# Seven products of 2x2 blocks in place of eight in half of the FFN's up projection

## The chip, the cores and the metric

The kernel runs on one core of a Trainium2 chip. The metric is device time in microseconds: from the first to the last instruction of the program on that core, lower is better. TensorE does the matrix products, VectorE and ScalarE work on elements and read the products out of PSUM, GpSimd does small moves, and SyncE (SP) issues most of the DMAs.

## What is computed

One layer of a hybrid causal decoder on 512 prompt tokens and 8 x 4 sample tokens, 544 in all, in fp32. The part that matters here is the last third of it, the ConvFFN:

```python
x = x + g1 * (jnp.concatenate([a_out, o], axis=-1) @ p['w_out'])
h2 = rms_norm(x, p['norm_ffn_g']) * (1 + sc2) + sh2
u, f_tail = causal_dwconv(f_prev, h2 @ p['w_up'], p['ffn_conv_w'], p['ffn_conv_b'])
gate, val = jnp.split(u, 2, axis=-1)
x = x + g2 * ((jax.nn.silu(gate) * val) @ p['w_down'])
```

`w_up` is 2048 x 11264, `w_down` 5632 x 2048, and the convolution has three taps along time.

## The kernel before

Channels lie on partitions, tokens on the free axis in two halves of 272 columns (256 of the prompt, 16 of the samples). A K tile is 128 input channels; the model width has 16. Every fp32 product is made of three fp32r products: `split` (L340) writes the rounded operand with ScalarE (hi) and the remainder with VectorE (lo), and `mm3` (L201) adds hi x hi, hi x lo and lo x hi in PSUM for both token halves, six matmuls of 128x128 weights and 272 columns. So a K tile of one output tile costs six matmuls.

Weights come through SP's queue in units of 512 KB: `load_w` (L190) fills one of three `raw_w` buffers with eight K tiles of an output tile, `split_w` (L195) splits four of them at once into `whi` and `wlo`, which have three buffers each. `mm_unit` (L208) is one load, two splits and 48 matmuls; `mm_pair_unit` (L219) does the same for four K tiles of two output tiles.

The FFN (from L840) has 44 pairs of tiles, gate tile f and value tile 44 + f. For each tile `up_conv` (L863) runs two units over the 16 K tiles into one accumulator of two banks, copies it to `us` with ScalarE (L874, L875), lets GpSimd copy the last columns to `tails`, and convolves: ScalarE makes `ca` (L879), VectorE adds two taps (L881). `up_pair` (L886) then applies SiLU to the gate tile, multiplies (L896, L902) and splits the result into `ahi` and `alo`, which the down projection reads. The first pair goes through `mm_pair_unit` over four units of a reordered copy `w_up0`, so that it uses each K tile of h2 as soon as it is there. The loop (L925 to L934) takes four pairs as a chunk. `down` (L908) for the chunk before stands behind the second pair of the next: eight loads, 16 output tiles of 24 matmuls, each added to x by `gated_add` (L332). The FFN's accumulators alternate between two pools, `ps_main` and `psf`, four buffers of two banks in all. `shift_cache` (L854) issues 128 copies of the attention cache from HBM to HBM on SP's queue, one behind every second load.

Between the output projection and the FFN (L827 to L837), the sum of squares becomes `rstd2`, each of the 16 K tiles goes through `modulated` (L324: a product on VectorE, scale and shift on ScalarE, two small steps on VectorE, hi on ScalarE, lo on VectorE), and the last `ada_stage` (L257) makes the gate of the FFN from 16 loads in `RAW_G` buffers.

The order in each engine's queue is not written out by hand: the framework lays the program out ahead of time with a model of the engines, and takes what comes first in the program where several instructions are ready. Queues run in that order on the chip.

Of the kernel before, what the change touches and what calls it, by code (L numbers as in the profile page):

```python
# [14 lines left out]
ALU = mybir.AluOpType  # L15
# [43 lines left out]
RAW_G = 7  # L59
# [59 lines left out]
def build(ctx, tc, A):  # L119
# [12 lines left out]
    hlp = pool("hlp")  # L132
    halfp = pool("halfp", bufs=2)
    ps_main = pool("ps_main", bufs=2, space=PSUM)
# [25 lines left out]
    # ------------------------------------------------------------ constants  # L160
# [25 lines left out]
    # ------------------------------------------------------------ weights  # L186
    def raw_tile():
        return wp.tile([P, 1024], F32, name="raw_s", bufs=RAW_S)
# [67 lines left out]
    # ------------------------------------------------------------ adaLN  # L256
# [39 lines left out]
    # ------------------------------------------------------------ norms  # L296
# [27 lines left out]
    def modulated(xk, rstd, sc, sh, hi, lo, xn):  # L324
        nc.vector.tensor_tensor(xn, xk, rstd, op=ALU.mult)  # L325
        nc.scalar.activation(pv(xn), pv(xn), AF.Identity, bias=modT[:, sh, 0:1], scale=modT[:, sc, 0:1])
        nc.vector.tensor_tensor(sv4(xn), sv4(xn), per_batch(modT[:, sc, 1:9]), op=ALU.mult)
        nc.vector.tensor_tensor(sv4(xn), sv4(xn), per_batch(modT[:, sh, 1:9]), op=ALU.add)
        nc.scalar.copy(hi, xn)
        nc.vector.tensor_tensor(lo, xn, hi.bitcast(F32), op=ALU.subtract)  # L330
# [19 lines left out]
    # ------------------------------------------------------------ norm and first projections  # L350
# [5 lines left out]
    b1 = mid.enter_context(ExitStack())  # L356
    wk = pool("wk", bufs=4, to=b1)
# [70 lines left out]
    # ------------------------------------------------------------ q, k, v and prompt attention  # L428
# [140 lines left out]
    # ------------------------------------------------------------ conv group  # L569
# [54 lines left out]
    # ------------------------------------------------------------ sample attention  # L624
# [147 lines left out]
    # ------------------------------------------------------------ output projection  # L772
# [34 lines left out]
    op = pool("op", bufs=4, to=o1)  # L807
    x2.append(half_tile())
    nc.scalar.dma_start(x2[1], A["xT"][:, 8:16])
    ssum2 = op.tile([P, 2, HALF], F32, name="ssum", bufs=1)  # L810

# [20 lines left out]
    h2hi, h2lo = hl_tiles()  # L832
    for k in range(KT):
        xn = op.tile([P, 2, HALF], F32, name="xn", bufs=XN)
        modulated(x2[k // 8][:, k % 8], rstd2, SC2 + k, SH2 + k, h2hi[:, k], h2lo[:, k], xn)
# [4 lines left out]
    fs = ctx.enter_context(ExitStack())  # L840
    psf = pool("psf", bufs=2, space=PSUM, to=fs)
# [4 lines left out]
    turn = [0]  # L846

    def ffn_ps():
        turn[0] += 1
        if turn[0] % 2:  # L850
            return main_ps()
        return psf.tile([P, 2, 512], F32, name="acc2")
# [10 lines left out]
    def up_conv(m, st_in, tails, slot, ps=None):  # L863
        if ps is None:
            ps = ffn_ps()
            for h in range(2):
                ins = mm_unit(ps, A["w_up"][m, h], h2hi, h2lo, 8 * h, h == 0, h == 1)
                if h:
                    shift_cache(ins)
# [4 lines left out]
        nc.scalar.copy(us[:, 2:USEG].rearrange("p (c n) -> p c n", c=2), pv(ps))  # L874
        nc.scalar.copy(us[:, USEG:].rearrange("p (c b w) -> p c b w", c=2, w=2 + DT)[:, :, :, 2:], sv4(ps))  # L875
# [10 lines left out]
    def up_pair(f, st_in, tails, j):  # L886
        pss = (None, None)
        if f == 0:
            pss = (ffn_ps(), ffn_ps())
            for q in range(4):  # L890
                mm_pair_unit(pss, A["w_up0"][q], h2hi, h2lo, 4 * q, q == 0, q == 3)
        gt = up_conv(f, st_in, tails, 2 * j, pss[0])
        vl = up_conv(FT + f, st_in, tails, 2 * j + 1, pss[1])
# [9 lines left out]
        hi = fp.tile([P, 2, HALF], F32R, name="ahi", bufs=6)  # L903
        lo = fp.tile([P, 2, HALF], F32R, name="alo", bufs=6)
# [3 lines left out]
    def down(c, last):  # L908
        for mp in range(8):
# [3 lines left out]
            for j in range(2):  # L913
                m = 2 * mp + j
                hi, lo = split_w(raw[:, j])
                ps = ffn_ps()
# [8 lines left out]
    for c in range(NCHUNK):  # L925
# [133 lines left out]
```

## Time and profile before

| | |
|---|---|
| median of 3 runs | 2702.55 us (2698.33 to 2708.47) |
| span of the profiled execution | 2703.5 us |
| TensorE busy | 2658.7 us (98%) |
| VectorE busy | 1353.2 us (50%) |
| ScalarE busy | 1026.9 us (38%) |
| GpSimd busy | 114.2 us (4%) |
| mean granted TensorE clock | 0.991 |

The page of the profile gives busy time of each engine and, in 40 slices of the span, its busy share. The chain of waits follows the work that ended last back through what released it. The views by line and shape give the mean duration of an instruction and the idle time of its engine before it; the timeline gives instructions in order of time, and the windows sum the engines' busy time in a stretch and show the granted clock there (1.00 is 2.4 GHz, 0.50 is 1.2 GHz).

### The profile page before, as it was taken

The page shows a single profiled execution, that of the slowest core. Times are in us where ns is not written, and L with a number is a line of the kernel's source. Part 1 is how long each engine was busy: PE and PEld are TensorE (multiplying, and loading weights), DVE is VectorE, ACT ScalarE, POOL GpSimd, SP SyncE. Part 2 cuts the span into 40 slices and gives each one's busy share as a digit, 9 for nine tenths or more (in the row PEclk, how much of TensorE's full clock was granted, in tenths as well). Part 3 has the DMA queues.
Part 4 walks back from the last instruction along what each step waited for, and adds up shares of the span by engine and source line. Part 5 has one row for each costly group of instructions (what it writes and reads, how often), then busy time and mean ns, then how long its engine had stood idle before and what let it go on. Part 6 is the DMA issues. An engine that isn't in the chain of part 4 may idle for free.

```text
span 2703.5 us, 51563 instructions
## 1 busy us (share of the span) xinstructions
PE 2658.7 (98%) x21601; PEld 2437.8 (90%) x21601; DVE 1353.2 (50%) x2584; ACT 1026.9 (38%) x1977; POOL 114.2 (4%) x448
## 2 busy tenths in 40 slices
PE   7999999999999999999999999999999999999999
PEld 5878677768777799799999999999999999999999
DVE  5678654744674243644444443444443534444444
ACT  4355454445446432533332323232323233332322
POOL 0000000000000000000000000000000000000000
PEclk8999999999999999999999999999999999999999
DMA  9874557676655442455555455454554555545544
GB/s 350 280 274 156 190 196 262 224 260 221 237 204 192 146 182 87 157 186 180 171 182 180 165 182 186 165 182 165 187 176 170 180 172 181 181 165 182 178 172 153
DMA packets 119129, 517.49 MB, mean 191 GB/s; under 512 B 15728, under 2 KB 25584, under 8 KB 116080
## 3 DMA queue, kind: packets, MB, share of 16 engines
q1 hardware_dynamic: 103744, 494.98, 52.6%
q10 hardware_dynamic: 15152, 19.22, 2.0%
q8 instruction: 169, 2.77, 0.4%
q14 instruction: 64, 0.52, 0.1%
HBM read 503.18 MB, written 144.92 MB: 240 GB/s over the span
## 4 chain that ended last, share of the span: by engine, by line
PE 96%; DMA 2%; DVE 1%; ACT 0%; issue 0%; ACTq 0%; DVEq 0%; SPq 0%
PE acc L205 85%; PE x L270 4%; PE x L701 2%; PE x L652 2%; DMA raw_s<-w_ada 1%; PE m L510 1%; PE m L440 1%; PE m L475 1%; PE m L472 1%; PE m L493 0%; PE acc L322 0%; DMA half<-xT 0%; DVE xn L325 0%; DMA raw_s<-kT_c 0%; PE m L502 0%; DMA small<-c_small 0%
## 5 line engine op out<-in xcount | busy, mean ns | idle before, releaser
L205 PE MATMUL acc<-hhi,whi 128*128 128x272 f32 x4608 | 975.0, 292 | 4.5 <-ACT hhi L341 2.3
L205 PE MATMUL acc<-hhi,wlo 128*128 128x272 f32 x4608 | 964.8, 290 | 0.0
L205 PE MATMUL acc<-hlo,whi 128*128 128x272 f32 x4608 | 961.5, 290 | 0.4 <-DVE hlo L330 0.2
L341 ACT CAST whi<-raw_w 128x512 fp32r<-128x512 f32 x752 | 466.2, 621 | 1304.1 <-PE acc L205 1256.5
L342 DVE TENSOR_TENSOR wlo<-raw_w,whi 128x512 fp32r<-128x512 f32 x752 | 517.6, 689 | 749.7 <-ACT whi L341 738.9
L205 PEld LDWEIGHTS acc<-hhi,whi 128*128 128x128 f32 x4608 | 724.9, 189 | 56.6 <-issue 40.0
L205 PEld LDWEIGHTS acc<-hlo,whi 128*128 128x128 f32 x4608 | 725.8, 189 | 22.9 <-issue 18.5
L205 PEld LDWEIGHTS acc<-hhi,wlo 128*128 128x128 f32 x4608 | 723.0, 189 | 22.6 <-issue 20.9
L205 PE MATMUL acc<-alo,whi 128*128 128x272 f32 x1408 | 292.0, 288 | 0.0
L205 PE MATMUL acc<-ahi,whi 128*128 128x272 f32 x1408 | 290.3, 287 | 0.0
L205 PE MATMUL acc<-ahi,wlo 128*128 128x272 f32 x1408 | 290.3, 287 | 0.0
L333 DVE SCALAR_TENSOR_TENSOR half<-acc,modT,half 128x512 f32<-128x512 f32 x200 | 150.2, 751 | 267.6 <-PE acc L205 267.0
L205 PEld LDWEIGHTS acc<-ahi,whi 128*128 128x128 f32 x1408 | 220.8, 188 | 0.0
L205 PEld LDWEIGHTS acc<-alo,whi 128*128 128x128 f32 x1408 | 220.7, 188 | 0.0
L205 PEld LDWEIGHTS acc<-ahi,wlo 128*128 128x128 f32 x1408 | 220.6, 188 | 0.0
L881 DVE SCALAR_TENSOR_TENSOR ca<-us,fw,ca 128x560 f32<-128x560 f32 x176 | 141.0, 801 | 75.9 <-ACT ca L879 73.2
L593 DVE SCALAR_TENSOR_TENSOR half<-g_p,cw,half 128x512 f32<-128x512 f32 x180 | 135.7, 754 | 3.1 <-ACT half L605 0.4
L270 PE MATMUL x<-raw_s,cin 128*9 128x128 f32 (+1 forms) x1920 | 118.3, 333 | 12.8 <-ACT cin L184 6.7
L270 PEld LDWEIGHTS x<-raw_s,cin 128*9 128x9 f32 x1920 | 48.9, 92 | 50.1 <-issue 9.9
L879 ACT ACTIVATE ca<-us,fw 128x560 f32<-128x560 f32 x88 | 75.3, 856 | 7.7 <-POOL us L873 1.1
L876 POOL COPY tails<-us 128x2 f32<-128x2 f32 x88 | 19.6, 222 | 1219.4 <-ACT us L874 1166.9
L398 DVE TENSOR_TENSOR part<-acc,part 128x544 f32<-128x544 f32 x64 | 46.2, 724 | 41.0 <-PE acc L205 40.9
(171 smaller groups left out, 1498.7 us busy)
## 6 DMA issues: line engine op xcount, KB each, us to landing
raw_s<-w_ada SPq DMA_DIRECT2D x176, 512.0 KB, 4.7
raw_w<-w_up SPq DMA_DIRECT2D x176, 512.0 KB, 3.5
o_k_s<-cache_k SPq DMA_DIRECT2D x64, 1022.0 KB, 7.8
o_v_s<-cache_v SPq DMA_DIRECT2D x64, 1022.0 KB, 7.4
raw_w<-w_down SPq DMA_DIRECT2D x88, 512.0 KB, 3.5
raw_w<-w_in SPq DMA_DIRECT2D x80, 512.0 KB, 4.4
raw_s<-kT_c SPq DMA_DIRECT2D x64, 448.0 KB, 4.2
raw_s<-v_c SPq DMA_DIRECT2D x56, 512.0 KB, 4.3
```

The lines of the kernel that those rows point to most:

```text
L205: nc.tensor.matmul(out[:, c, 0:HALF], lhsT=w, rhs=x[:, c, :], start=start and i == 0, stop=stop and i == 2)
L270: nc.tensor.matmul(ps[32 * j:32 * j + 9, 0:w], lhsT=silc[:, kt, :], rhs=t[:, c:c + w], start=kt == 0, stop=kt == KT - 1)
L333: nc.vector.scalar_tensor_tensor(pv(dst), pv(ps), modT[:, gate, 0:1], pv(dst), op0=ALU.mult, op1=ALU.add)
L341: nc.scalar.copy(hi, src)
L342: return nc.vector.tensor_tensor(lo, src, hi.bitcast(F32), op=ALU.subtract).ins
L398: nc.vector.tensor_tensor(part[:, t], halves(ps), part[:, t], op=ALU.add)
L440: nc.tensor.matmul(s_ps[:, 0:HALF], lhsT=blk, rhs=sq[:, c, :], start=True, stop=True)
L593: nc.vector.scalar_tensor_tensor(pa, win(j), cw[:, i, j:j + 1], pa, op0=ALU.mult, op1=ALU.add)
L652: nc.tensor.matmul(s_ps[32 * g:32 * g + 32, 0:hk], lhsT=qb[:, 2 * g + o, n, :], rhs=ks[g], start=o == 0 and n == 0, stop=o == 1 and n == 1 ...
L701: nc.tensor.matmul(o_ps[32 * g:32 * g + 32, :], lhsT=pT[0:w, c0:c0 + 32], rhs=rhs[g], start=kt == 0, stop=kt == 7)
L879: nc.scalar.activation(acc, us[:, 0:UN], AF.Identity, bias=fw[:, m, 3:4], scale=fw[:, m, 0:1])
L881: nc.vector.scalar_tensor_tensor(acc, us[:, j:j + UN], fw[:, m, j:j + 1], acc, op0=ALU.mult, op1=ALU.add)
```

## The change

For the first eight K tiles of h2, a pair is read as a product of 2x2 blocks: rows are the gate and the value tile, the inner index is the K group (tiles 0 to 3, tiles 4 to 7), columns are the token halves. The four blocks of weights a11, a12 (gate), a21, a22 (value) and the four of h2 are combined so that seven block products do (Winograd's form of Strassen's scheme). The combinations of h2, t1 to t4, are made once ahead of the FFN and split into seven blocks `shi`/`slo`; those of the weights (s1, s2, s4 and a11 - a21) are made by VectorE in each pair. K tiles 8 to 15 are multiplied directly as before, with the two token halves' matmuls no longer alternating one by one but three by three.

A product is 12 matmuls into one bank. The seven use five one-bank accumulators (b1 to b5, from four buffers in `psf`): b1 and b2 are read out after their first product and go on accumulating. The parts p1, u2 and u3 are made from them in SBUF, and `place` writes the sums into `us`: ScalarE copies the gate's first half, VectorE adds for the other three. The down projection keeps `ps_main` alone, two accumulators. `down` for the chunk before now stands behind the first pair of the next chunk, `ahi` and `alo` have five buffers in place of six, and `RAW_G` is 4 in place of 7. The first pair takes K tiles 8 to 15 through `mm_pair_unit` with two units, its seven products after that, and adds the two. The pools for h2's tiles, `raw_s` and `op` are opened and closed at other places. The diff, cut to its core:

```diff
-RAW_G = 7
+RAW_G = 4
+Q = 4
...
-    op = pool("op", bufs=4, to=o1)
+    op = pool("op", bufs=4, to=o1, side="right")
...
-    h2hi, h2lo = hl_tiles()
-    for k in range(KT):
+    hs.close()
+    hf = pool("hf", to=fs)
+    h2hi, h2lo = (hf.tile([P, KT - 2 * Q, 2, HALF], F32R, name=n) for n in ("dhi", "dlo"))
+    sthi, stlo = (hf.tile([P, 7, Q, HALF], F32R, name=n) for n in ("shi", "slo"))
...
+    for k in range(2 * Q, KT):
+        modulate2(k, h2hi[:, k - 2 * Q], h2lo[:, k - 2 * Q])
     run(ada_stage(psm, op, len(FIRST) + 7, get=raw_g))
+    for j in range(Q):
+        x1, x2nd = modulate2(j, None, None), modulate2(Q + j, None, None)
+        b11, b12, b21, b22 = x1[:, 0], x1[:, 1], x2nd[:, 0], x2nd[:, 1]
+        tt = op.tile([P, 4, HALF], F32, name="tt", bufs=1)
+        t1, t2, t3, t4 = (tt[:, i] for i in range(4))
+        nc.vector.tensor_tensor(t1, b12, b11, op=ALU.subtract)
+        nc.vector.tensor_tensor(t2, b22, t1, op=ALU.subtract)
+        nc.vector.tensor_tensor(t3, b22, b12, op=ALU.subtract)
+        nc.vector.tensor_tensor(t4, b21, t2, op=ALU.subtract)
+        split(sthi[:, 0, j], stlo[:, 0, j], b11)
+        split(sthi[:, 1:3, j], stlo[:, 1:3, j], x2nd)
+        split(sthi[:, 3:7, j], stlo[:, 3:7, j], tt)
...
-    psf = pool("psf", bufs=2, space=PSUM, to=fs)
+    psf = pool("psf", bufs=4, space=PSUM, to=fs)
...
+    def mm1(out, whi, wlo, xhi, xlo, start, stop):
+        for i, (w, x) in enumerate(((whi, xhi), (whi, xlo), (wlo, xhi))):
+            nc.tensor.matmul(out[:, 0:HALF], lhsT=w, rhs=x, start=start and i == 0, stop=stop and i == 2,
+                             skip_group_check=True)
+
+    def product(out, w, i, start, stop):
+        hi, lo = split_w(w)
+        for j in range(Q):
+            mm1(out, hi[:, j], lo[:, j], sthi[:, i, j], stlo[:, i, j], start and j == 0, stop and j == Q - 1)
+
+    def direct(outs, raw, starts, stops):
+        for u in range(2):
+            hi, lo = split_w(raw[:, u])
+            for a in range(4):
+                k = 4 * u + a
+                for c in range(2):
+                    mm1(outs[c], hi[:, a], lo[:, a], h2hi[:, k, c], h2lo[:, k, c],
+                        starts[c] and k == 0, stops[c] and k == 7)
+
+    def place(us, c, op, ps, t=None):
+        prompt = us[:, 2 + HP * c:2 + HP * (c + 1)]
+        sample = us[:, USEG:].rearrange("p (c b w) -> p c b w", c=2, w=2 + DT)[:, c, :, 2:]
+        op(prompt, ps[:, 0:HP], t and t[:, 0:HP])
+        op(sample, ps[:, HP:HALF].rearrange("p (b t) -> p b t", t=DT),
+           t and t[:, HP:HALF].rearrange("p (b t) -> p b t", t=DT))
...
+    def up_mm(f, usg, usv, early):
+        g0, _ = load_w(A["w_up"][f, 0])
+        v0, ins = load_w(A["w_up"][FT + f, 0])
+        shift_cache(ins)
+        a11, a12, a21, a22 = g0[:, 0], g0[:, 1], v0[:, 0], v0[:, 1]
+        s1, s2, s4 = (fp.tile([P, 4, P], F32, name="sum", bufs=3) for _ in range(3))
+        b1 = bank()
+        product(b1, a11, 0, True, True)
+        nc.vector.tensor_tensor(s1, a21, a22, op=ALU.add)
+        nc.vector.tensor_tensor(s2, s1, a11, op=ALU.subtract)
+        b2 = bank()
+        product(b2, s2, 4, True, True)
+        p1 = part_tile("p1")
+        nc.scalar.copy(p1, b1[:, 0:HALF])
+        u2 = part_tile("u2")
+        plus(u2, b2[:, 0:HALF], p1)
+        product(b1, a12, 1, False, early)
+        nc.vector.tensor_tensor(a21, a11, a21, op=ALU.subtract)
+        product(b2, a21, 5, False, True)
+        u3 = part_tile("u3")
+        plus(u3, b2[:, 0:HALF], p1)
+        b4 = None
+        if not early:
+            b4 = bank()
+            g1, _ = load_w(A["w_up"][f, 1])
+            direct((b1, b4), g1, (False, True), (True, False))
+        place(usg, 0, copied, b1)
+        b3 = bank()
+        product(b3, s1, 3, True, True)
+        plus(u2, b3[:, 0:HALF], u2)
+        nc.vector.tensor_tensor(s4, a12, s2, op=ALU.subtract)
+        if early:
+            b4 = bank()
+        product(b4, s4, 2, early, True)
+        place(usg, 1, plus, b4, u2)
+        b5 = bank()
+        product(b5, a22, 6, True, early)
+        if not early:
+            v1, ins = load_w(A["w_up"][FT + f, 1])
+            shift_cache(ins)
+            direct((b5, b3), v1, (False, False), (True, True))
+        place(usv, 1, plus, b3, u3)
+        place(usv, 0, plus, b5, u3)
...
-                ps = ffn_ps()
+                ps = main_ps()
...
-            if c and j == 1:
+            if c and j == 0:
                 down(c - 1, False)
```

## Rows read from the trace of the kernel before

**Rows 1.** The page: TensorE's busy time, and its busy tenths in slices.

```profile
PE 2658.7 (98%) x21601; PEld 2437.8 (90%) x21601; DVE 1353.2 (50%) x2584; ACT 1026.9 (38%) x1977; POOL 114.2 (4%) x448
...
PE   7999999999999999999999999999999999999999
```

**Rows 2.** Chain of waits: start, length in us, engine, tile, line, instructions.

```profile
717.01 1.85 PE x L701 x16
...
1128.84 1570.60 PE acc L205 x12528
```

**Rows 3.** Window of the FFN: length, busy of PE, PEld, DVE, ACT, POOL, clock, DMA.

```profile
1138.00:2699.00 1561.00, 1561.00 (x12457) 1561.00 (x12457) 703.05 (x1350) 504.57 (x870) 77.00 (x350) 1.00 0.51 175
```

**Rows 4.** Groups by line and shape: busy us, mean ns, idle before. TensorE.

```profile
L701 PE MATMUL x<-raw_s,t2k 128*32 128x512 f32 x224 | 45.4, 602 | 0.0
```

**Rows 5.** Timeline between two pairs: start, length in us. VectorE, then ScalarE.

```profile
1762.44 1.64 DVE L881 SCALAR_TENSOR_TENSOR ca<-us,fw,ca 128x560 f32<-128x560 f32 x2 [0.83 <-ACT ca L879]
1763.99 0.69 DVE L342 TENSOR_TENSOR wlo<-raw_w,whi 128x512 fp32r<-128x512 f32 x1
1764.60 0.68 DVE L896 TENSOR_TENSOR a<-ca 128x512 f32<-128x512 f32 x1
...
1766.10 0.73 DVE L342 TENSOR_TENSOR alo<-a,ahi 128x544 fp32r<-128x544 f32 x1 [0.71 <-ACT ahi L341]
1766.93 0.69 DVE L342 TENSOR_TENSOR wlo<-raw_w,whi 128x512 fp32r<-128x512 f32 x1
...
1760.26 0.62 ACT L341 CAST whi<-raw_w 128x512 fp32r<-128x512 f32 x1 [2.39 <-PE acc L205]
1760.79 0.58 ACT L874 COPY us<-acc 128x512 f32<-128x512 f32 x1
```

**Rows 6.** Groups by line and shape, VectorE and ScalarE.

```profile
L445 DVE SCALAR_TENSOR_TENSOR w<-m,w 128x272 f32<-128x272 f32 x32 | 12.6, 434 | 16.6 <-ACT w L443 16.5
...
L902 DVE TENSOR_TENSOR a<-ca 128x32 f32<-128x32 f32 x44 | 8.0, 181 | 0.0
...
L879 ACT ACTIVATE ca<-us,fw 128x560 f32<-128x560 f32 x88 | 75.3, 856 | 7.7 <-POOL us L873 1.1 <-POOL tails L877 0.4
L874 ACT COPY us<-acc 128x512 f32<-128x512 f32 x88 | 51.1, 581 | 4.1 <-DMA st_in<-state_f 4.1
...
L504 ACT COPY t2k<-m 128x256 f32<-128x256 f32 x8 | 3.0, 371 | 9.4 <-PE m L502 9.4
```

**Rows 7.** DMA issues by line: KB each, median us from issue to landing.

```profile
raw_w<-w_up SPq DMA_DIRECT2D x176, 512.0 KB, 3.5
o_k_s<-cache_k SPq DMA_DIRECT2D x64, 1022.0 KB, 7.8
```

**Rows 8.** Timeline of a down step, VectorE: the large step of a gated add.

```profile
1703.32 0.75 DVE L333 SCALAR_TENSOR_TENSOR half<-acc,modT,half 128x512 f32<-128x512 f32 x1 [1.47 <-PE acc L205]
```

**Rows 9.** Timeline ahead of the FFN: VectorE's first and last, TensorE's first.

```profile
1100.16 2.00 DVE L325 TENSOR_TENSOR xn<-half,rstd 128x544 f32<-128x544 f32 x3
...
1134.34 0.73 DVE L330 TENSOR_TENSOR hlo<-xn,hhi 128x544 fp32r<-128x544 f32 x1 [0.77 <-ACT hhi L329]
...
1104.48 0.82 PE L205 MATMUL acc<-hhi,whi 128*128 128x272 f32 x2
```

**Rows 10.** Windows, columns as in rows 3.

```profile
400.00:450.00 50.00, 49.81 (x424) 33.65 (x422) 26.36 (x47) 23.01 (x52) 3.28 (x10) 1.00 0.77 262
...
750.00:800.00 50.00, 45.34 (x357) 34.17 (x358) 34.58 (x59) 22.12 (x51) 4.95 (x8) 0.93 0.64 217
...
1100.00:1105.00 5.00, 3.58 (x26) 0.91 (x27) 4.02 (x13) 3.85 (x6) 0.00 (x0) 0.57 0.64 260
1105.00:1110.00 5.00, 4.61 (x29) 3.09 (x27) 4.34 (x14) 3.69 (x6) 0.00 (x0) 0.75 0.00 2
```

**Rows 11.** Timeline of SP's queue: the second half of the last adaLN loads.

```profile
1091.09 4.60 SPq L265 DMA_DIRECT2D raw_g<-w_ada  x8
```

More of the change, by code (lines that the diff above doesn't have):

```diff
@@ L131, in build @@
     wp = pool("wp")
-    hlp = pool("hlp")
     halfp = pool("halfp", bufs=2)
+    hs = ExitStack()
+    hlp = pool("hlp", to=hs)
     ps_main = pool("ps_main", bufs=2, space=PSUM)
@@ L187, in raw_tile @@
     def raw_tile():
-        return wp.tile([P, 1024], F32, name="raw_s", bufs=RAW_S)
+        return rs.tile([P, 1024], F32, name="raw_s", bufs=RAW_S)
     def load_w(src):
@@ L328, in modulated @@
         nc.vector.tensor_tensor(sv4(xn), sv4(xn), per_batch(modT[:, sh, 1:9]), op=ALU.add)
+        if hi is None:
+            return
         nc.scalar.copy(hi, xn)
@@ L356, in build @@
     b1 = mid.enter_context(ExitStack())
+    rs = pool("rs", to=b1)
     wk = pool("wk", bufs=4, to=b1)
@@ L810, in build @@
     ssum2 = op.tile([P, 2, HALF], F32, name="ssum", bufs=1)
+    fs = ctx.enter_context(ExitStack())
     def rest():
@@ L845, in build @@
     copies = [(n, b, i) for n in "kv" for b in range(DB) for i in range(8)]
[L846 to L852, printed above, removed]
     def shift_cache(ins, n=1):
@@ L861, in shift_cache, with bank @@
                         A[f"cache_{name}"][b, DT * DC + i * D2D:DT * DC + (i + 1) * D2D].rearrange("(p f) -> p f", p=P))
-    def up_conv(m, st_in, tails, slot, ps=None):
-        if ps is None:
-            ps = ffn_ps()
[L866 to L869, printed above, removed]
+    def bank():
+        return psf.tile([P, 512], F32, name="b")
+    def mm1(out, whi, wlo, xhi, xlo, start, stop):
+        for i, (w, x) in enumerate(((whi, xhi), (whi, xlo), (wlo, xhi))):
+            nc.tensor.matmul(out[:, 0:HALF], lhsT=w, rhs=x, start=start and i == 0, stop=stop and i == 2,
+                             skip_group_check=True)
@@ new lines, in place, with plus, copied @@
+    def place(us, c, op, ps, t=None):
[4 more added lines that the diff above has]
+           t and t[:, HP:HALF].rearrange("p (b t) -> p b t", t=DT))
+    def plus(out, ps, t):
+        nc.vector.tensor_tensor(out, ps, t, op=ALU.add)
+    def copied(out, ps, t):
+        nc.scalar.copy(out, ps)
@@ new lines, in part_tile @@
+    def part_tile(name):
+        return fp.tile([P, HALF], F32, name=name, bufs=1)
+    def up_mm(f, usg, usv, early):
[41 more added lines that the diff above has]
+        place(usv, 0, plus, b5, u3)
@@ L870, in up_conv, with us_tile @@
+    def us_tile(st_in, slot):
         us = fp.tile([P, UW], F32, name="us", bufs=2)
@@ L873, in up_conv @@
         nc.gpsimd.tensor_copy(seg[:, :, 0:2], st_in[:, slot])
-        nc.scalar.copy(us[:, 2:USEG].rearrange("p (c n) -> p c n", c=2), pv(ps))
-        nc.scalar.copy(us[:, USEG:].rearrange("p (c b w) -> p c b w", c=2, w=2 + DT)[:, :, :, 2:], sv4(ps))
+        return us
+    def up_conv(m, us, tails, slot):
+        seg = us[:, USEG:].rearrange("p (b w) -> p b w", w=2 + DT)
         nc.gpsimd.tensor_copy(tails[:, slot, 0, :], us[:, SEQ:SEQ + 2])
@@ L886, in up_pair @@
     def up_pair(f, st_in, tails, j):
[L887 to L893, printed above, removed]
+        usg, usv = us_tile(st_in, 2 * j), us_tile(st_in, 2 * j + 1)
+        early = f == 0
+        if early:
+            pss = (main_ps(), main_ps())
+            for q in range(2):
+                mm_pair_unit(pss, A["w_up0"][q], h2hi, h2lo, 4 * q, q == 0, q == 1)
+        up_mm(f, usg, usv, early)
+        if early:
+            for us, ps in zip((usg, usv), pss):
+                for out, src in ((us[:, 2:USEG].rearrange("p (c n) -> p c n", c=2), pv(ps)),
+                                 (us[:, USEG:].rearrange("p (c b w) -> p c b w", c=2, w=2 + DT)[:, :, :, 2:], sv4(ps))):
+                    nc.vector.tensor_tensor(out, src, out, op=ALU.add)
+        gt = up_conv(f, usg, tails, 2 * j)
+        vl = up_conv(FT + f, usv, tails, 2 * j + 1)
         nc.scalar.activation(gt, gt, AF.Silu)
@@ L902, in up_pair @@
         nc.vector.tensor_tensor(sv4(a), smp(gt), smp(vl), op=ALU.mult)
-        hi = fp.tile([P, 2, HALF], F32R, name="ahi", bufs=6)
-        lo = fp.tile([P, 2, HALF], F32R, name="alo", bufs=6)
+        hi = fp.tile([P, 2, HALF], F32R, name="ahi", bufs=5)
+        lo = fp.tile([P, 2, HALF], F32R, name="alo", bufs=5)
         split(hi, lo, a)
@@ L986 @@
     w_out0 = pair_units(I["w_out"][0], np.array([[0, 1]]))[0]
-    w_up0 = pair_units(I["w_up"][0], np.array([[0, FT]]))[0]
+    w_up0 = pair_units(I["w_up"][0], np.array([[0, FT]]))[0, 2:4]
     wa = I["w_ada"][0].reshape(KT, P, 96, P)
```

6 lines of the change are left out of this document (3 added, 3 removed).

## The prediction

> **What bounds the kernel now.** I read the page's head first: TensorE is busy for 98% of the span, in every slice after the first, and VectorE for half of it [rows 1]. Busy alone doesn't prove a bound, so I took the chain of waits next: from 1128.84 us to the end it is one unbroken run of TensorE, 12528 matmuls in 1570.60 us [rows 2]. That is 1570.60 / 12528 = 125.37 ns from one matmul to the next, which is the price of a matmul here; the 288 ns that a single one lasts is its whole way through the array and overlaps its neighbours. From 1138 to 2699 us TensorE is never idle at granted clock 1.00, while VectorE works 703.05 and ScalarE 504.57 of 1561 us [rows 3]. So in the FFN a matmul less is 125 ns less, as long as the other engines keep up. From the code the FFN has 88 x 96 = 8448 up and 11 x 16 x 24 = 4224 down matmuls.
>
> **Matmuls removed.** A pair (one gate and one value tile) costs 192 matmuls now. After, its first eight K tiles cost seven products of 12 (four K tiles, three hi/lo terms, one token half), 84 in place of 96; the other eight stay at 96. So 180 per pair, 12 x 0.12537 = 1.504 us less, over 44 pairs 66.2 us. Each matmul still has its own weight load and 272 columns. What changes is the order: in a product all 12 go to one PSUM bank, in the direct part three in a row do, where now two banks alternate. No row has same-column accumulation into one bank back to back; the nearest is the attention output, 512 columns each, 16 of them into one bank in 1.85 us [rows 2, 4], so I take nothing extra, and keep the other end as a rival.
>
> **Work added per pair on VectorE.** Issue to issue a 512-column split takes 0.61 us (1763.99 to 1764.60), and an FFN-convolution step 0.72 us, from (1763.99 - 1762.44 - 0.1) / 2 [rows 5]. Added are three lo splits and four weight sums at 0.61 (the same two-operand form), 4.3 us; three 272-column sums out of PSUM, each bounded by the 128x272 row with 0.43 us alone [rows 6], about 0.36 in a queue, 1.1 us; three placements at 0.33 + 0.10, estimated from the same row and from the 32-column one [rows 6], 1.3 us. Together 6.7 us a pair, 290 us in all: VectorE goes from 703 to about 990 of some 1540 us. ScalarE gains three casts at about 0.53, one copy out of PSUM at 0.37 and two half-size ones, and loses the four copies that it makes out of the accumulators now [rows 5, 6]: some 1 us a pair. Neither becomes the bound on throughput. That cover holds on average; the question is the places where a product of only 1.50 us follows another.
>
> **The tight spot, walked through.** Call the end of a pair's last matmul 0. The next pair runs P1 (a11 into b1), P2 (s2 into b2), P3 (a12 into b1), P4 (a11 - a21 into b2), each 1.50, then two direct halves D1 and D2 of 3.01, P5 to P7, and D3 and D4. P4 could issue at 3 x 1.504 - 0.29 = 4.22. It needs the sum u2 read out of b2, after P2 ends at 3.01, and its own hi/lo split; the three hi/lo buffers let that split begin only when P1 ends at 1.50. Just then the last pair's tail is due, for its value tile is complete only at 0: four placements on VectorE 0.03 to 0.97, ScalarE's scaling of the tile (0.86 us [rows 6]) 1.0 to 1.86, two convolution steps on VectorE 1.9 to 3.4, the product of the halves 0.7, the lo split of the result. ScalarE does the hi cast of P4 only after that scaling and the copy of b1, 2.2 to 2.85. VectorE at 3.4: u2 (to 3.75), then either P4's lo (done at 4.4, a stall of about 0.15) or first the product of the halves (lo done at 5.1, a stall of 0.9). The order is the planner's; the rows show both kinds, a next weight split ahead of the product of the halves at 1763.99 and behind it at 1766.93 [rows 5]. I take 0.6 us, nearer the upper end because the product of the halves comes earlier in the program. A stall can't be negative, for there is no idle time to win. Between pairs with a down step between them VectorE has 3.01 us for each split, and I take nothing; so it counts at 3 + 10 x 3 = 33 transitions: 33 x 0.6 = 20 us, between 3 and 30.
>
> The other products have slack: b1 must be copied to p1 between 1.50 and 2.72, and is by 2.2; the splits for P5, P6, P7 and the direct halves each have 3 us or more for about 1.5 us of work. **Loads:** all four of a pair pass the same SP queue with the same two cache copies, but the value tile a22 is held until P7's split (D2 ends at 12.0, so about 13.3), so the next pair's first value tile is loaded only then, for sums that P2 needs by 23.8. A weight load lands in 3.5 us, a cache copy in 7.8 [rows 7]; with 2.7 us for two sums and a split it is ready at 19.5, or at 23.8 behind a copy. Nothing, or at most 0.5 us.
>
> Here a rule of the Trainium skill speaks against the change: Perfetto Trace Analysis, Optimizing Tensor Performance, Matmuls, says that independent matmul groups should rotate through different PSUM banks, so that evacuating one overlaps the next group. P3 and P4 take up b1 and b2 again after one product. If both evacuations stood open, 0.37 + 0.43 us in 44 pairs [rows 6], some 35 us, in place of the 20 taken for the transitions, the sum below would be 2690; my walk hides most of that behind P2 and P3.
>
> **Down step.** It gets two accumulators in place of four. Its gated add starts as the group ends and is through with the bank 0.9 us later (0.75 [rows 8], then a small step of 0.18 like the 32-column row [rows 6]), while the buffer is wanted 3.0 us later. Nothing; moving the down step from behind the second pair to behind the first costs nothing by itself, and sets the 33 above.
>
> **The start of the FFN.** Now the 16 K tiles of h2 are made from 1100.16 to 1135.07 us, 34.9 us with the first weight splits among them, 2.2 us a tile; TensorE begins the FFN at 1104.48 and keeps close behind [rows 9]. By 1128.84 it has 12672 - 12528 = 144 done, so the first pair's 192 end at 1134.9. After: tiles 8 to 15 come first, 8 x 2.2 us, to about 1117.6, and feed 96 direct matmuls (12 us). The others need four batches; VectorE per batch: two products 1.28, four small ones 0.40, four differences of 272 columns 1.45, lo splits of 272, 544 and 1088 columns 2.2, at 0.64 us per 544 columns, (2.00 - 0.72) / 2 [rows 9], 5.3 us; four are 21.3, to 1138.9, and with weight sums between them I take 1141. Nothing else is there for TensorE, since every product needs all four batches: then 66 matmuls remain, 8.3 us, and its clock will have fallen: around the present gap, with TensorE waiting for 1.4 us of five, the granted clock was 0.57, then 0.75 [rows 10]; I add 2 us. The first pair ends at 1151 in place of 1134.9: 16 us later, between 10 (sums fit in gaps, no clock loss) and 24 (the batch runs as one chain of 7.3 us). The last adaLN stage keeps four loads ahead in place of seven: three more of the eight that now take 1091.09 to about 1103.5 [rows 11, 10], some 5 us more, ends at about 1109, before the products that follow it; nothing. Memory pools that move or close earlier add no instruction.
>
> **Sum**, against the span of 2703.5 (0.95 above the median of the runs, so I treat them as one): the 43 pairs behind the first save 64.7, the first ends 16 later, transitions 20: 2703.5 - 64.7 + 16.2 + 20 = **2675 us**. Own range: 2703.5 - 64.7 + 10 + 3 = 2652 to 2703.5 - 64.7 + 24 + 30 = 2693.
>
> **Rivals.** *All covered* (a little below 2652): the planner fits P4's split ahead everywhere and the first pair loses under 10 us. For it: VectorE stays near 65%. Against: the batches are VectorE work with nothing beside it. *Two open spots*: P4 waits 0.9, and 0.5 for the late value tile: 33 x 1.4 = 46 with 24 at the start: 2709, so from 2693 to 2716. For it: the long hold of a22; against: loads land in 3.5 us. *The tail ahead of P4, slower than before*: if VectorE's queue has the whole tail, with the lo split that waits for ScalarE's cast of the result, ahead of u2 and of P4's lo, these come at 5.9 to 7.0 in place of 4.22, and P4 waits 2.8 us at 33 transitions, 92 us: 2703.5 - 64.7 + 16.2 + 92 = 2747. It decides from 33 x 1.85 = 61 us on (2716). For it: program order; against: that lo split has waited for its cast while the queue stood [rows 5], and the planner did put a weight split between the convolution and the product. *The matmuls no longer come at 125.37 ns*, as one bank is written 12 times running, or, from the gaps, at a lower clock: 66.2 us / 7920 up matmuls, so 8.4 ns each eats the whole gain, about 2740. For the bank no row speaks. For the clock: from 750 to 800 us, with 4.7 us idle, it was 0.93, from 400 to 450, with 0.2 us idle, 1.00 [rows 10]; gaps of 0.6 us are nearer the second.
>
> **How the numbers follow.** Forecast 0.64, all covered 0.06, two open spots 0.17, tail ahead 0.09, slower matmuls 0.04. This kernel's measurements can tell about 0.5% from no change, 2689 and 2716 us. Faster is 0.06 and 0.60 of the forecast's 0.64: 0.66. Same is the rest, 0.04 and 0.17: 0.21. Slower 0.13. The range takes the forecast's own and most of the open spots: 2650 to 2712.
>
> **What would show it.** Right: in the FFN 12144 matmuls; TensorE at 125.4 ns inside products; gaps of 0.1 to 0.9 us ahead of P4, put down to VectorE, at 33 places, none after a down step; a first pair that ends near 1151 us, with TensorE largely idle from about 1118 to 1139 and VectorE full there. Wrong: gaps elsewhere in the pair, waits on loads of w_up, a wider step between matmuls, a wait of ScalarE's p1 copy, or a chain in which VectorE carries the steady part.

## The result, and the profile after

The changed kernel takes 2669.19 us, the median of four runs (2663.86 to 2669.57), where the kernel before took 2704.17 us in its four (2698.33 to 2708.47): a ratio of 0.9867, with an interval of 0.9854 to 0.9879, 1.3% faster. 2675 had been predicted. The span of its profiled execution is 2667.8 us, 35.7 less than before's 2703.5. The total hides that three terms of the sum were wrong, in both directions, as the rows show.

The page of after, busy time by engine and the two TensorE lines in 40 slices (beside [rows 1]):

```profile
PE 2603.1 (98%) x21073; PEld 2380.3 (89%) x21073; DVE 1655.6 (62%) x3312; ACT 1082.9 (41%) x2069; POOL 163.4 (6%) x448
...
PE   6999999999999999789999999999999999999999
PEclk8999999999999999899999999999999999999999
```

TensorE has 528 matmuls less (21601 to 21073), 12 for each of 44 pairs, as the diff says. VectorE has 728 instructions and 302 us more; 290 had been estimated. New is the dent in the slices just before the middle: the start of the FFN.

The chain of waits of after, from the output projection on (start, length, what):

```profile
956.06 132.48 PE acc L207 x1056
1089.15 7.43 DMA raw_g<-w_ada
...
1157.13 88.13 PE b L887 x696
...
1342.36 42.61 PE b L887 x336
...
1433.62 90.50 PE b L887 x718
1524.13 45.28 PE acc L207 x360
...
1572.66 90.50 PE b L887 x718
...
2621.15 42.53 PE acc L207 x336
```

The one run of 12528 matmuls of [rows 2] is now cut, but few of the cuts are waits. From one chunk to the next, 1433.62 to 1572.66, are 139.04 us for 4 x 180 up and 384 down matmuls: 125.94 ns each, where before had 125.37. Inside, the 718 of the up rows take 90.51 us, 126.06 ns each; the rest, 386, take 48.53, 125.7 each.

Windows of after: length, busy of PE, PEld, DVE, ACT, POOL, granted clock, DMA share, GB/s. First the start of the FFN, then the steady part (beside [rows 3, 10]):

```profile
1115.00:1120.00 5.00, 5.00 (x42) 5.00 (x41) 4.93 (x13) 2.32 (x4) 0.00 (x0) 1.00 0.02 5
1120.00:1125.00 5.00, 2.25 (x17) 1.82 (x15) 4.97 (x13) 2.85 (x6) 0.00 (x0) 1.00 0.00 0
1125.00:1130.00 5.00, 1.41 (x3) 0.79 (x3) 5.00 (x13) 4.49 (x7) 0.00 (x0) 0.60 0.00 0
1130.00:1135.00 5.00, 1.42 (x3) 0.79 (x3) 4.13 (x13) 2.97 (x5) 0.00 (x0) 0.50 0.00 0
1135.00:1140.00 5.00, 0.00 (x0) 0.00 (x0) 3.80 (x7) 1.20 (x2) 0.00 (x0) 0.50 0.00 0
1140.00:1145.00 5.00, 2.35 (x9) 2.19 (x10) 4.89 (x8) 2.05 (x4) 1.37 (x4) 0.50 0.24 62
1145.00:1150.00 5.00, 5.00 (x36) 5.00 (x35) 3.11 (x6) 2.12 (x5) 0.00 (x0) 0.85 0.88 314
...
1160.00:2660.00 1500.00, 1498.47 (x11893) 1497.03 (x11892) 980.99 (x2027) 549.85 (x946) 122.62 (x343) 1.00 0.52 181
```

From 1120 to 1140 us TensorE is busy for 5.1 us of 20, and then stands until 1142.65; VectorE works 17.9 of the same 20 us. From 1160 on TensorE is idle for 1.5 us of 1500, with VectorE at 65%.

**Where the 35.7 us are.** The second pair's first matmul starts at 1153.7, worked back from 1157.13: a gap of 0.40, and 24 matmuls. Before, the first pair ended at 1134.9. Seen from the start of the output projection's unbroken run of 1056 matmuls (958.00 before, 956.06 after), that is 197.6 against 176.9 us: the first pair ends 20.7 later. The code ahead of that run does the same work, and three kernels in which it is that of before start the run at 954.4 to 958.0 (before and the two of the step experiments below), so I don't put its 1.9 us down to the change. After the first pair, 43 x 12 matmuls less are 64.7; the five gaps that are left hold 2.6; the wider step costs 0.79 ns x 7740 up and 0.2 ns x 4224 down matmuls, 7.0. The up step before is read from the starts of the first of 768 up matmuls and of the first down matmul behind them, (1543.62 - 1447.41) / 768 = 125.27 ns; the down step was 125.5:

```profile
1447.41 0.41 PE L205 MATMUL acc<-hhi,whi 128*128 128x272 f32 x2
...
1543.62 0.41 PE L205 MATMUL acc<-ahi,whi 128*128 128x272 f32 x2
```

Together -64.7 + 20.7 - 1.9 + 2.6 + 7.0 = -36.3; 0.6 stay unassigned.

### The profile page after: what moved, and what is told of

The parts are those of the page before. It is cut to its first block, busy times and chain, and to the rows that moved or that the text cites. A ratio compares the mean times of both kernels' runs of the same rounds, so it can differ in the third digit from the quotient of the medians.

```text
span 2667.8 us, 51885 instructions
## 1 busy us (share of the span) xinstructions
PE 2603.1 (98%) x21073; PEld 2380.3 (89%) x21073; DVE 1655.6 (62%) x3312; ACT 1082.9 (41%) x2069; POOL 163.4 (6%) x448
## 4 chain that ended last, share of the span: by engine, by line
PE 95%; DVE 2%; DMA 2%; ACT 1%; issue 0%; DVEq 0%; ACTq 0%
PE acc L207 47%; PE b L887 36%; PE x L272 4%; PE x L706 2%; PE x L657 2%; PE m L515 1%; PE m L445 1%; DMA raw_s<-w_ada 1%; PE m L480 1%; PE acc L324 1%; PE m L477 1%; PE m L498 1%; DMA raw_g<-w_ada 0%; DVE slo L346 0%; DVE qkr L320 0%
## 5 line engine op out<-in xcount | busy, mean ns | idle before, releaser
L207 PE MATMUL acc<-hhi,whi 128*128 128x272 f32 x1792 | 393.1, 298 | 2.7 <-ACT hhi L345 2.3
L887 PE MATMUL b<-dhi,whi 128*128 128x272 f32 x1376 | 394.7, 289 | 0.0
L887 PE MATMUL b<-dlo,whi 128*128 128x272 f32 x1376 | 392.8, 288 | 0.0
L887 PE MATMUL b<-dhi,wlo 128*128 128x272 f32 x1376 | 384.3, 289 | 0.0
L207 PE MATMUL acc<-hhi,wlo 128*128 128x272 f32 x1792 | 382.6, 292 | 0.0
L207 PE MATMUL acc<-hlo,whi 128*128 128x272 f32 x1792 | 380.4, 292 | 0.0
L887 PE MATMUL b<-shi,whi 128*128 128x272 f32 x1232 | 358.5, 291 | 17.0 <-ACT whi L345 8.4
L207 PEld LDWEIGHTS acc<-hhi,whi 128*128 128x128 f32 x1792 | 282.5, 189 | 53.2 <-issue 39.6
L207 PEld LDWEIGHTS acc<-hhi,wlo 128*128 128x128 f32 x1792 | 283.0, 190 | 22.4 <-issue 20.9
L207 PEld LDWEIGHTS acc<-hlo,whi 128*128 128x128 f32 x1792 | 283.2, 189 | 21.0 <-issue 18.5
```

The source lines that it names most:

```text
L207: nc.tensor.matmul(out[:, c, 0:HALF], lhsT=w, rhs=x[:, c, :], start=start and i == 0, stop=stop and i == 2)
L887: nc.tensor.matmul(out[:, 0:HALF], lhsT=w, rhs=x, start=start and i == 0, stop=stop and i == 2, skip_group_check=True)
```

## The experiments

Each time below is the median with its ratio to runs of the kernel before on the same chip. Since the part ahead of the output projection varies by some 7 us among kernels that share it (its run starts at 951.3 to 958.0), I also give the profiled span from the start of that run, "the rest": 1745.5 us before, 1711.7 after.

### Where the new pools lie

The sums s1, s2, s4 and the parts are in `fp`, whose memory `op` held until the last batch. The first kernel gives them memory of their own, with a smaller RAW_G to make room; the second changes RAW_G alone.

```diff
-RAW_G = 4
+RAW_G = 2
...
+    fe = pool("fe", to=fs)
...
-        return fp.tile([P, HALF], F32, name=name, bufs=1)
+        return fe.tile([P, HALF], F32, name=name, bufs=1)
...
-        s1, s2, s4 = (fp.tile([P, 4, P], F32, name="sum", bufs=3) for _ in range(3))
+        s1, s2, s4 = (fe.tile([P, 4, P], F32, name="sum", bufs=3) for _ in range(3))
```

> The changed kernel with the weight sums (s1, s2, s4) and the parts p1, u2, u3 in memory of their own, in place of memory that the last norm's work buffers held before; RAW_G is 2 in place of 4 to make room. Theory A: part of the first pair's delay is this reuse of memory: the first weight sum starts at 1140.5 us, right behind the last step that reads the old buffers, and TensorE stands from 1134.3 to 1142.7 with two thirds of the blocks of h2 ready. With memory of their own the sums run among the batches, P2 and others go ahead with the batches that are there, and the kernel gains 3 to 6 us on the changed kernel (2669): 2663 to 2666, with TensorE idle for less than 4 us in that place. Rival B: VectorE's queue is full with the batches up to 1140.5 anyway, and sums put among them delay them: within 1.5 us of the changed kernel.

> The control for the run before: the changed kernel with RAW_G 2 in place of 4 and nothing else. Theory: the last adaLN stage ends ahead of the products that follow it, so two loads fewer ahead cost nothing: within 1.5 us of the changed kernel (2669). Rival: the stage is on the path through the PSUM banks that the FFN takes over from it (in the changed kernel the first product starts at 1122.6, right behind its last step), so 2 to 5 us slower than the changed kernel.

Measured: 2670.18 us (0.9879, 0.9862 to 0.9896), the rest 1714.0; the control 2670.04 (0.9875, 0.986 to 0.989), the rest 1713.5. Neither gains. First after, then the kernel with its own memory, VectorE's timeline (start, length):

```profile
1139.21 1.29 DVE L346 TENSOR_TENSOR slo<-tt,shi 128x1088 fp32r<-128x1088 f32 x1 [1.16 <-ACT shi L345]
1140.53 0.69 DVE L928 TENSOR_TENSOR sum<-raw_w 128x512 f32<-128x512 f32 x1
```

```profile
1129.08 0.67 DVE L929 TENSOR_TENSOR sum<-raw_w 128x512 f32<-128x512 f32 x1
...
1146.75 1.29 DVE L346 TENSOR_TENSOR slo<-tt,shi 128x1088 fp32r<-128x1088 f32 x1 [0.57 <-ACT shi L345]
```

In after the first sum starts as the last batch's split ends. Seen from the start of the run of 1056, the first sum stands 10 us earlier with memory of its own, and the last split 9 us later (7 later than in the control): what VectorE does for the weights it does not do for the batches. So the wait for memory is real, and takes nothing from the end: VectorE has both pieces of work to do, in either order.

### The batches without their differences

```diff
-        tt = op.tile([P, 4, HALF], F32, name="tt", bufs=1)
-        ... (t1 to t4)
-        split(sthi[:, 3:7, j], stlo[:, 3:7, j], tt)
...
         hi, lo = split_w(w)
+        i = i % 3
```

> The changed kernel without t1 to t4: the four differences and their split are left out of each batch, and the four products that used them take other blocks, so part of the computation is missing; the matmuls keep their number and order. Theory: the batches are bound by VectorE, and a batch loses 4 x 0.36 + 1.21 = 2.65 us of it, so the first pair ends some 10 us earlier: 2657 to 2661, and TensorE idle between 1120 and 1145 falls by about 10 us. Rival: a chain (norm, scale on ScalarE, small steps, difference, cast, remainder) sets the batch, or the wait behind it: less than 5 us gained, 2664 or more.

Measured: 2655.04 us (0.9818, 0.9798 to 0.9837), the rest 1702.7, 9.0 less than after. Windows of this kernel, columns as above:

```profile
1125.00:1130.00 5.00, 1.27 (x4) 0.95 (x4) 4.13 (x10) 2.65 (x6) 0.14 (x2) 0.50 0.21 60
1130.00:1135.00 5.00, 5.00 (x28) 4.84 (x28) 3.09 (x7) 1.55 (x4) 1.22 (x2) 0.66 0.87 317
```

TensorE is full again from 1130, where after takes until 1145. The start is bounded by the batches, as the theory had it. Whether by the amount of VectorE's work or by the length of a batch's chain this run can't tell: it takes the differences, ScalarE's cast of them and their remainder out of both.

### P4 without matmuls ahead of it

In after's trace no P4 waits in the steady part. TensorE around one P4:

```profile
1482.99 0.29 PE L887 MATMUL b<-shi,wlo 128*128 128x272 f32 x1
1483.12 0.29 PE L887 MATMUL b<-dhi,whi 128*128 128x272 f32 x1
1483.24 0.29 PE L887 MATMUL b<-dlo,whi 128*128 128x272 f32 x1
1483.37 0.29 PE L887 MATMUL b<-dhi,whi 128*128 128x272 f32 x1
1483.49 0.29 PE L887 MATMUL b<-dlo,whi 128*128 128x272 f32 x1
1483.62 0.29 PE L887 MATMUL b<-shi,whi 128*128 128x272 f32 x1
```

Four direct matmuls (`dhi`, `dlo`), later in the program, stand between P3 and P4. VectorE in the same place:

```profile
1481.09 0.69 DVE L346 TENSOR_TENSOR wlo<-raw_w,whi 128x512 fp32r<-128x512 f32 x1
1481.69 0.80 DVE L978 SCALAR_TENSOR_TENSOR ca<-us,fw,ca 128x560 f32<-128x560 f32 x1
1482.40 0.44 DVE L912 TENSOR_TENSOR u<-b,p 128x272 f32<-128x272 f32 x1
1482.76 0.68 DVE L346 TENSOR_TENSOR wlo<-raw_w,whi 128x512 fp32r<-128x512 f32 x1
1483.35 0.69 DVE L1000 TENSOR_TENSOR a<-ca 128x512 f32<-128x512 f32 x1
```

TensorE uses the lo tiles in the order in which VectorE makes them: the trace has 884 such splits and 884 groups of matmuls that read them, and paired in order none is read before its split has ended. By that order P4's lo is the split of 1481.09, ahead of the convolution's second step and of u2, and ready at 1481.78; the one of 1482.76, behind u2, belongs to the direct half. The experiment holds the direct half back behind P4:

```diff
-        product(b2, a21, 5, False, True)
+        p4 = product(b2, a21, 5, False, True)
...
-            direct((b1, b4), g1, (False, True), (True, False))
+            with tc.issue_after(p4):
+                direct((b1, b4), g1, (False, True), (True, False))
```

> The changed kernel with one order more: in each pair the direct matmuls of the gate tile stand behind P4 in TensorE's queue. Theory: the wait of P4 for its remainder is there as the prediction walked it, but the planner fills it with the first direct matmuls (four of them ahead of P4 at 1483.12 us in the changed kernel, 0.5 us). Without them P4 waits 0.3 to 0.6 us at the 33 pairs that follow a pair directly: 10 to 20 us slower than the changed kernel (2669), 2679 to 2689, with gaps put down to VectorE ahead of P4. Rival: the four are only taken because they are ready, and P4 would have waited for nothing: within 2 us of the changed kernel.

Measured: 2667.98 us (0.9869, 0.9849 to 0.989), no change; the expected cost did not come. Its timeline, TensorE and VectorE at the one P4 of a chunk that waits:

```profile
1506.50 0.36 PE L887 MATMUL b<-shi,whi 128*128 128x272 f32 x1 [0.21 <-DVE u L914]
...
1506.82 0.30 PE L887 MATMUL b<-shi,wlo 128*128 128x272 f32 x1
...
1504.60 0.69 DVE L346 TENSOR_TENSOR wlo<-raw_w,whi 128x512 fp32r<-128x512 f32 x1 [0.40 <-ACT whi L345]
...
1505.92 0.43 DVE L914 TENSOR_TENSOR u<-b,p 128x272 f32<-128x272 f32 x1
1506.28 0.68 DVE L346 TENSOR_TENSOR wlo<-raw_w,whi 128x512 fp32r<-128x512 f32 x1
```

P4 starts at 1506.50, once u2 is done (1505.92 + 0.43 = 1506.35). Its lo, the split of 1504.60, has been there since 1505.29; the split of 1506.28 is the direct half's and ends, at 1506.96, only after P4's first matmul that reads `wlo` has started (1506.82). In all 44 pairs of both traces P4's lo is ready before P3's last matmul starts, by 0.24 us or more. What can come late is u2: in the first pair of ten chunks it ends 0.35 us after that start, and there P4 waits. Such a gap comes once in a chunk: 139.4 us for 139.0. By that period the filling in after is worth some 4 us in 11 chunks, too little for the medians to show; the rest of the 20 was never there.

### The step between matmuls: one bank, a busier VectorE

Both edits are to the kernel before. First, the up units write 12 matmuls in a row to one bank:

```diff
+            for c in range(2):
+                for a in range(4):
+                    for i, (w, x) in enumerate(((hi, xhi), (hi, xlo), (lo, xhi))):
...
-                ins = mm_unit(ps, A["w_up"][m, h], h2hi, h2lo, 8 * h, h == 0, h == 1)
+                ins = mm_unit_bank(ps, A["w_up"][m, h], h2hi, h2lo, 8 * h, h == 0, h == 1)
```

> The kernel before with another order of the matmuls in the up projection's units, and nothing else: for each four K tiles first the 12 matmuls of one token half, all into one bank, then the 12 of the other, where the kernel before alternates between the two halves one by one. In the changed kernel an up matmul takes 126.0 ns against 125.3 in the kernel before. Theory: that comes with accumulating into one bank several times running: 126.0 to 126.2 ns here too, 8256 x 0.7 = 6 us slower than the kernel before. Rival: the pace is that of the stretch with more VectorE and ScalarE work beside it, not of the order: 125.3 ns, no change.

Measured: 2705.27 us beside 2703.71 (1.0005, 0.9992 to 1.0018). Its chain of waits, an up stretch and a down step:

```profile
2459.65 96.22 PE acc L227 x768
2555.87 48.20 PE acc L205 x384
```

96.22 / 768 = 125.29 ns; before had 125.27. One bank costs nothing. Second, ten more VectorE instructions of 512 columns in a pair, on a scratch tile:

```diff
+        for _ in range(5):
+            nc.vector.tensor_tensor(extra, extra, extra, op=ALU.max)
         return acc
```

> The kernel before with ten more VectorE operations per pair of the FFN (512 columns each, on a scratch tile that nothing else reads), which brings VectorE's share in the FFN from 45% to about 63%, that of the changed kernel; nothing else is changed and no matmul depends on them. It tells where the wider step of the changed kernel's up matmuls comes from (126.0 ns against 125.3), after accumulating into one bank turned out to cost nothing. Theory: more work on the other engines beside it widens the step: 125.8 to 126.2 ns in the up projection here, some 5 us slower than the kernel before. Rival: the step stays at 125.3 ns and the time at that of the kernel before (within 0.2%): then it is something in the changed kernel's own matmul stream.

Measured: 2704.67 beside 2703.85 (0.9999, 0.999 to 1.0009). Its window in an up stretch, and its chain:

```profile
1460.00:1540.00 80.00, 80.00 (x641) 80.00 (x640) 73.61 (x117) 29.24 (x51) 13.01 (x26) 1.00 0.49 168
...
1125.48 1570.61 PE acc L205 x12528
```

VectorE is at 92% there, and the step stays at 125.37 ns. So neither suspect makes the 126.06 of after. Nor is it a sum of waits: of after's 11268 steps between 1190 and 2610 us all but eight are 119 to 131 ns long, so the increase lies in the ordinary steps. Its cause stays open.

### The first pair without products

If the first pair does not wait for all four batches, TensorE can work beside them. Here the pair goes direct over all 16 K tiles: K tiles 8 to 15 as in after, K tiles j and 4 + j as soon as batch j is there, with b12 split as an eighth block (h12, l12). The weights `w_up0` become four reordered units; RAW_G is 3.

```diff
+    ps0 = (main_ps(), main_ps())
+    for q in range(2):
+        mm_pair_unit(ps0, A["w_up0"][q], h2hi, h2lo, 4 * q, q == 0, False)
     for j in range(Q):
...
+        h12, l12 = (op.tile([P, HALF], F32R, name=n, bufs=2) for n in ("h12", "l12"))
+        split(h12, l12, b12)
+        if j % 2 == 0:
+            raw0, _ = load_w(A["w_up0"][2 + j // 2])
+        ... (24 matmuls into ps0)
         split(sthi[:, 3:7, j], stlo[:, 3:7, j], tt)
...
-        up_mm(f, usg, usv, early)
         if early:
-            ... (add the direct half to us)
+            ... (copy ps0 to us)
+        else:
+            up_mm(f, usg, usv, early)
```

> The changed kernel with the first pair multiplied directly over all 16 K tiles, as in the kernel before (192 matmuls in place of 180), each of its first eight K tiles as soon as its batch has it; one block more of h2 is split per batch for that, and RAW_G is 3. The other 43 pairs keep their seven products. Theory: the loss at the start is TensorE's idle time while the batches are made, with 72 matmuls of the first pair left behind the last batch; given direct work it uses 4 x 24 matmuls of that time, and only the last few stay behind: the first pair ends 8 to 10 us earlier, 2659 to 2661. Rival: the extra splits and casts on VectorE and ScalarE (0.36 us and four weight splits of 0.6 us) push the batches back by as much: 2666 or more.

Measured: 2661.87 us (0.985, 0.9832 to 0.9868), the rest 1705.6, 6.1 less than after. Windows:

```profile
1130.00:1135.00 5.00, 4.87 (x35) 4.24 (x34) 5.00 (x13) 2.85 (x5) 0.00 (x0) 1.00 0.00 0
...
1140.00:1145.00 5.00, 0.89 (x5) 0.57 (x3) 3.67 (x6) 1.93 (x4) 0.31 (x3) 0.50 0.12 30
```

TensorE works among the batches, at clock 1.00 until it has to wait again, and VectorE, which has another split in each batch, ends them later. Still 6 us are won, for none of the first pair remains behind the batches. With one `tt`, a batch can't write its differences until the split of the last batch has read it. Two edits with two: e7 also takes RAW_G to 2, e10 takes h12 and l12 to one buffer instead.

```diff
-        tt = op.tile([P, 4, HALF], F32, name="tt", bufs=1)
+        tt = op.tile([P, 4, HALF], F32, name="tt", bufs=2)
```

> The kernel with a direct first pair (run e6_first_direct, 2662) with two buffers in place of one for the differences t1 to t4, and RAW_G 2 in place of 3 to make room. Theory: at the end the batches run as a chain, since the differences of the last batch wait until the remainder of those before has been read (VectorE waits 1.2 us at 1137.3 and 1.2 us at 1141.9 in e6_first_direct); with two buffers 2 to 3 us are gained: 2659 to 2660. Rival: VectorE's amount of work alone sets the end of the batches: within 1 us.

> The kernel with a direct first pair (e6_first_direct, 2662) with two buffers in place of one for the differences, with RAW_G 3 as there; room is made by one buffer in place of two for the extra block of h2. In e7_first_direct_tt2, with RAW_G 2, the adaLN loads stood ahead of the first pair's weights in SP's queue, so that run could not tell. Theory: the last batch's differences no longer wait for the remainder of those before: 1 to 3 us faster than e6_first_direct, 2659 to 2661. Rival: VectorE's amount of work sets the end of the batches, and the single buffer of the extra block adds a wait: within 1 us of e6_first_direct or slower.

Measured: e7 2665.72 (0.9862, 0.9847 to 0.9877), the rest 1708.4, slower than with one `tt`: in its trace SP issues weights of the first pair only at 1128.95, behind the adaLN loads that wait for two buffers. So e7 says nothing on `tt`. e10, with RAW_G still 3: 2658.95 us (0.984, 0.9824 to 0.9857; 2654.92 to 2664.36), the rest 1701.7: 3.9 less than with one `tt` and 10.0 less than after. Its median is the lowest of the kernels that compute everything, though its interval just touches after's and overlaps that of one `tt`; the 3.9 rest on one profile of each. The last differences' split, first with one `tt` (e6), then e10:

```profile
1141.93 1.29 DVE L346 TENSOR_TENSOR slo<-tt,shi 128x1088 fp32r<-128x1088 f32 x1 [1.17 <-ACT shi L345]
```

```profile
1136.49 1.29 DVE L346 TENSOR_TENSOR slo<-tt,shi 128x1088 fp32r<-128x1088 f32 x1 [0.53 <-ACT shi L345]
```

Seen from the run of 1056 (952.96 and 951.28) these are 189.0 and 185.2 us: the last split starts 3.8 earlier, as much as the rest gained.

If VectorE's work bounds the batches, GpSimd could take part of it: the four differences (on top of e7; the first is shown), or the product with `rstd2` of half the tiles (on top of the first of these kernels):

```diff
-        nc.vector.tensor_tensor(t1, b12, b11, op=ALU.subtract)
+        nc.gpsimd.tensor_tensor(t1, b12, b11, op=ALU.subtract)
...
-        x1, x2nd = modulate2(j, None, None), modulate2(Q + j, None, None)
+        x1, x2nd = modulate2(j, None, None), modulate2(Q + j, None, None, nc.gpsimd)
```

> The run before (e7_first_direct_tt2) with the four differences of each batch made by GpSimd in place of VectorE. Theory: the batches are bound by VectorE's work, 4 x 4 x 0.36 = 5.8 us of which goes to an engine that is idle there; a difference of 272 columns takes GpSimd an estimated 0.75 us (1.48 us for 544 in the kernel before), so 3 us a batch beside VectorE's 4.5: 3 to 5 us faster than e7_first_direct_tt2. Rival: the longer chain of a batch (1.5 us more) eats it, or GpSimd and VectorE slow each other: no gain or a loss up to 4 us.

> e6_first_direct with one of the two products x * rstd of each batch made by GpSimd in place of VectorE. Unlike the differences, which GpSimd took 0.78 to 1.16 us for and which stand in the middle of a batch's chain (e8_first_direct_gp: no gain), this product stands at its head and can be made ahead. Theory: 4 x 0.64 = 2.6 us less on VectorE, 1 to 2.5 us gained on e6_first_direct: 2659.5 to 2661. Rival: GpSimd's 1.5 us or more comes on top of the chain, as the three buffers of the norm's product allow little work ahead: 0 to 4 us slower than e6_first_direct.

Measured: 2667.51 (0.9865, 0.9848 to 0.9883) against e7's 2665.72, and 2664.85 (0.9855, 0.9841 to 0.987) against 2661.87: 1.8 and 3.0 us more, within the intervals, and no gain. Groups of the first of the two by line and shape (busy us, mean ns, idle before):

```profile
L862 POOL TENSOR_TENSOR tt<-xn 128x272 f32<-128x272 f32 x4 | 4.6, 1157 | 0.0
```

These four are the slowest of the four kinds of difference, 1.16 us in the mean (single ones take 0.77 to 1.81 us), where 272 columns cost VectorE 0.43 [rows 6]; the kernel's last split of them starts at 1150.94, where e7's starts at 1146.60. So less work on VectorE won nothing when it came with a longer chain; how much of that is the chain and how much GpSimd slowed by its neighbour is not told apart.

## Why the prediction came out right, step by step

**Matmuls removed: right.** 528 less, and 64.7 us behind the first pair, at before's step.

**The step: wrong, 7.0 us for nothing.** The step grew to 126.06 ns in the up stretches. The rival had the size of the risk (8.4 ns would eat the gain; 0.79 came) but not its cause: one bank costs nothing, shown, and neither does a busy VectorE. What does is not known.

**Work added on VectorE: right.** 302 us for 290; 65% in the FFN, and no throughput bound.

**P4: wrong, 20 us where none came.** The step that failed is the order on VectorE. The walk put P4's lo split behind both convolution steps and u2, ready at 4.4 or 5.1 us of the pair; the planner put it ahead of the second convolution step and of u2, and it is ready before P3's last matmul starts in all 44 pairs. That leaves u2, late in one pair of a chunk, some 4 us in all as the kernel without filling shows. And the walk let P4 start with nothing else to run: the planner had four direct matmuls to put there in 33 pairs, which hides even that. The rival *all covered* held for this term. What waits is P3 for the copy p1, which the prediction called safe: in three of 44 pairs, gaps of 0.40, 0.55 and 0.47 us, the larger part of the 2.6. Waits of after from 1150 to 2660 us (waiter, what it waits for: us in total, times, longest us):

```profile
PE b L887 <- ACT p L933: 0.9, 3, 0.4
DVE sum L928 <- DMA raw_w<-w_up: 32.5, 42, 2.0
```

The second line is the load of the next pair's first value tile, which the rival *two open spots* feared: VectorE does wait for it, 32.5 us, and TensorE never does. The rule of the Trainium skill (Perfetto Trace Analysis, Optimizing Tensor Performance, Matmuls) that groups should rotate through banks would have given 2690, as the prediction priced it from rows; with banks taken up again after one product the trace shows three waits of about half a microsecond, so here it is nearly free, other matmuls being there to run.

**The first pair: right in kind, 20.7 us for 16.2, inside its 10 to 24.** The batches ended at 1140.5, as worked out (1141), with TensorE idle and VectorE full. The error lies behind them. I had TensorE do the remaining 66 matmuls in 8.3 us and 2 for the clock. In the trace:

```profile
1133.87 0.43 PE L887 MATMUL b<-shi,wlo 128*128 128x272 f32 x1
1142.65 0.59 PE L887 MATMUL b<-shi,whi 128*128 128x272 f32 x1 [8.36 <-ACT whi L345]
```

TensorE stood 8.36 us and went on only 2.15 after the last batch, for s1, s2 and their split came no earlier; then six products were left, 72 matmuls in 11.05 us (1142.65 to 1153.7) for the 10.3 allowed, the first of them 0.22 us apart at granted clock 0.50. With batches that ended 1.4 later as seen from the run of 1056, this makes the 4.5, but for 0.2. "Memory pools that move or close earlier add no instruction" was true and not enough: they add a wait, for the sums. That wait alone costs nothing (the first experiment), since the weight work that VectorE does behind the batches would otherwise stand among them.

**Down step, loads, RAW_G: right.** No down step waits for an accumulator but the last, where nothing else is left to run: its gaps are 0.47 us, for the last pair's hi, and 0.69, for a gated add. TensorE never waits for `w_up`, and RAW_G 2 for 4 leaves the time where it was. The last adaLN stage, though, ended at 1122.5 us, not at about 1109, and P1 started right behind it, at 1122.64; that costs nothing here because the batches end later still.

So the total came as close as it did by luck: 20 - 2.6 = 17.4 us charged too much met 4.5 + 7.0 = 11.5 charged too little, and the run ahead of the FFN gave 1.9 that I don't put down to the change. Of the prediction's own signs of being wrong two came, the wider step and a wait for the p1 copy, and of its signs of being right the gaps ahead of P4 did not.

## What to carry to other kernels

A start that needs every input before its first product turns hidden preparation into idle time: let the first piece of work use the plain form while the combinations for the others are made (here worth 6 to 10 us of the 20.7). When a wait is walked through by hand, ask of each operand where the planner may put the work that makes it, the earliest place among them, and which later work is ready to fill the hole. Where one engine is nearly full, read the chain as well as the busy time: giving the weight sums memory of their own only moved work about, a second buffer in the batches' chain let the last split start 3.8 us earlier, and work handed to a slower engine won nothing.

## What the runs showed of the hardware

A matmul of the same form and size comes at 125.27 ns in one stream and at 126.06 in another, at the same granted clock of 1.00; twelve in a row into one bank (125.29) and VectorE at 92% (125.37 in all) do not make the difference. A difference of 272 columns took GpSimd 0.78 to 1.16 us in the mean of four, beside a busy VectorE. With TensorE busy for 1.4 us of five twice over, then for none, then for 2.4, the granted clock was 0.60 and then 0.50 up to 1145 us, and 0.85 in the next five, which TensorE filled.
